# Weights of narrow products 64 bytes further in their buffers, buffers at two places mod 512, and one buffer for a norm's two values

## The chip, the cores and the metric

One NeuronCore of one Trainium2 chip. The metric is the device time of one execution in microseconds, lower is better; it is compared with the same kernel without the change, on the same chip.

## The reference

A trunk of two decoder layers over 512 tokens of width 1024, all in float32, batch 1, then a final RMS norm:

```python
def hybrid_layer(x, g_mix, w_in, sinks, w_a, w_b, w_out, g_mlp, w_up, w_down):
    h = rmsnorm(x, g_mix)
    z = h @ w_in                                   # (512, 1024) @ (1024, 4864)
    aq, ak, av, rq, rk, rv, rg, ga, gb = jnp.split(z, SPLIT_POINTS, axis=-1)
    ...
    ya = sliding_window_sink_attention(aq, ak, av, sinks) @ w_a
    ...
    r = chunkwise_retention(rq, rk, rv)
    ...                                            # per-head norm, swish gate
    yb = r.astype(x.dtype) @ w_b
    mixed = jax.nn.sigmoid(ga) * ya + jax.nn.sigmoid(gb) * yb
    x = x + mixed @ w_out
    h2 = rmsnorm(x, g_mlp)
    x = x + jnp.square(jax.nn.relu(h2 @ w_up)) @ w_down      # width 4096 inside
    return x
```

## The kernel before

**Products.** The activations stand transposed in SBUF: features on the 128 partitions, tokens along the free axis. Every float32 operand is split into two parts, `hi` (rounded to float32r) and `lo` (the rest), and a product is three matmuls, hi x hi, hi x lo and lo x hi, accumulated in one PSUM bank (`products`, lines 390 to 392; `wo` has its own three-matmul loop, line 1296). A matmul has a stationary operand of 128x128, which a separate weight load (PEld) brings into the array, and a moving operand of 128 partitions and 512 or 256 columns.

**Units of weights.** Weights come from HBM in units of 128 x 1024 float32. `load_until` loads a unit into a `raw` buffer (five of them), `split_until` splits it: ScalarE writes `hi` (line 338), VectorE writes `lo` (line 339). There are four `hi` and four `lo` buffers, taken in turn; `unit` keeps up to three units split ahead of the one in use. `unit_order` names the units in their order: `w_in`, `w_a`, `rv`, `w_b`, `wo`, `w_up`, `pair`, `block`, and at the very end `w_end`.

**Which width a unit serves.** Units of `w_in`, `w_a`, `w_b` and `w_up` are stationary, in slices of 128 columns, against 512 moving columns (`chunk`, `group`, `two_chunks`, the loop over `w_a`). Units of `rv`, `block` and `w_end` are themselves the moving operand, 512 columns at a time. Units of `wo` and `pair` are stationary against 256 moving columns: `output` (`wo`) and `pair` (the up projection but its first 512 columns) use a seven-product scheme over 2x2 halves, in which the moving operand is one half of the tokens. `pair` runs seven `multiply` calls of 4 x 3 matmuls, and two pairs stand behind one another, 168 matmuls of 256 columns; then comes `down` with 84 matmuls of 512 columns on `block` units. There are 14 pairs to a layer. `output` runs 7 x 48 matmuls of 256 columns to a layer.

**Where things lie in SBUF.** The pools follow one another and each tag has its place for the whole kernel. Byte addresses in a partition, from the allocation:

| tile | begins at | mod 512 | bytes |
|---|---|---|---|
| `x`, `xh`, `xl`, `r0` to `r7`, `ones`, ... | 2,176 and on | 128 | |
| `raw`, 5 buffers | 119,424 | 128 | 4,096 each |
| `hi`, 4 buffers | 139,904 | 128, all four | 4,096 each |
| `lo`, 4 buffers | 156,288 | 128, all four | 4,096 each |
| `acc` (pool `tmp`) | 172,672 | 128 | 2,048 |
| `t`, `sh`, `sl` | 174,720 | 128 | 2,048 each |
| `rstd` | 193,152 | 128 | 2,048 |
| `big`, 6 buffers | 195,200 | 128 | 4,096 each |
| small tiles; `columns` is the last but one | 219,776 | various | |
| `late` | 220,224 | 64 | 8,192 |

(The first value of `x`, 2,176, is a header of small values; the activations start 512 bytes on.) A weight slice of 128 columns is 512 bytes, a moving slice of 256 columns 1,024, so within a buffer all slices of 256 or 512 columns keep the buffer's place mod 512. `xh`, `xl`, the `r` tiles and `late` hold moving operands; the `r` tiles and `late` are dealt out in quarters by `Slots`. `late` is used again and again: as a ninth `r` tile in the first half of a layer, and for other things later.

**The two values of a norm.** `acc` is the sum of squares over the features, written by `squared_input` and read by `token_sums` on TensorE (line 561); `rstd` is the inverse root spread over the partitions, written by ScalarE in `Rms.finish` (line 609) and read by VectorE where results leave PSUM, last in `gate` (line 826). Each has a buffer of its own.

**What sets the order.** Each engine has its own queue, and waits on semaphores that the framework places from the tiles; SP issues the weight loads, POOL the sums of weights in DRAM and the adds to `y`. TensorE's order is that of the program: `unit` is called by the product that needs it and splits further ones ahead.

Of the kernel before, what the change touches and what calls it, by code (L numbers as in the profile page):

```python
# [10 lines left out]
F32 = mybir.dt.float32  # L11
F32R = mybir.dt.float32r
# [5 lines left out]
P = 128  # L18
T = 512
# [3 lines left out]
NB = T // P  # L23
# [21 lines left out]
N_BLOCK = 8  # L45
N_PAIR = 14
UNIT = 1024
WARM = 8
PACE = 0.8
DEEP = 3  # L50
# [2 lines left out]
SPLIT = 3  # L53
# [57 lines left out]
def view(slot):  # L111
    return slot[0][:, slot[1], :]
# [3 lines left out]
def decoder(ctx, tc, xT, x_first, w_in, w_rv, w_a, w_b, w_wo, w_up, w_pair, w_down, w_end, tables, decay, band, g_last, out):  # L116
# [4 lines left out]
    wpool = ctx.enter_context(tc.tile_pool(name="wpool", bufs=3))  # L121
    tmp = ctx.enter_context(tc.tile_pool(name="tmp", bufs=6))
    small = ctx.enter_context(tc.tile_pool(name="small", bufs=6))
# [4 lines left out]
    def f32(ap):  # L128
        return ap.bitcast(F32)
# [7 lines left out]
    def bank(pool, name):  # L137
        return pool.tile([P, T], F32, tag=pool.name, name=name)
# [27 lines left out]
    def halves(i):  # L166

        return (slice(0, UNIT // 2), slice(UNIT // 2, UNIT)) if i < 3 else (slice(0, UNIT),)

    def raw_tile():  # L170
        return wpool.tile([P, UNIT], F32, tag="raw", name="raw", bufs=5)

# [7 lines left out]
    def load_until(n):  # L180
        while state["loaded"] < min(n, len(order)):
            i = state["loaded"]
            layer, name, j = order[i][:3]
            if name == "pair":
                load_part(i)
            elif name == "block":
                load_block(i)
            elif name in MIXING:
                load_values(i)
            else:  # L190
                raws[i] = raw_tile()
                for at in halves(i):
                    queue = nc.scalar if i == 0 and at.start == 0 else nc.sync
                    source = w_end[j] if name == "w_end" else weights[name][layer, j]
                    queue.dma_start(raws[i][:, at], source[:, at])
                    if i < 3:
                        load_x()
            state["loaded"] += 1
# [3 lines left out]

    LEFT, RIGHT = slice(0, UNIT // 2), slice(UNIT // 2, UNIT)

    sums_up = [dram.tile([N_PAIR, P, UNIT], F32, name=f"sums_up{l}") for l in range(DEPTH)]
    sums_down = [dram.tile([N_BLOCK, P, 2 * UNIT], F32, name=f"sums_down{l}") for l in range(DEPTH)]
    sums_last = dram.tile([P, 2, UNIT], F32, name="sums_last")
    MIXING = {"rv": w_rv, "wo": w_wo}
# [67 lines left out]
    def add_part(i):  # L276
        if order[i][3] in (1, 2):
            last = raws.pop(i - 1)
            at = LEFT if order[i][3] == 1 else RIGHT
            nc.vector.tensor_tensor(raws[i][:, at], last[:, LEFT], last[:, RIGHT], ALU.add)  # L280
# [18 lines left out]
    def add_block(i):  # L299
        e, part = order[i][2:]  # L300
        if part in (2, 4) and e < N_BLOCK - 1:
            raws[i] = raws.pop(i - 2)
            nc.vector.tensor_tensor(raws[i], raws[i], raws.pop(i - 1), ALU.add)
# [10 lines left out]
    def add_values(i):  # L314
        part = order[i][2]
        if part in (2, 4):
            raws[i] = raws.pop(i - 2)
            nc.vector.tensor_tensor(raws[i], raws[i], raws.pop(i - 4), ALU.add)

    def split_until(n):  # L320
        while state["split"] < min(n, len(order)):
            i = state["split"]
            name, part = order[i][1], order[i][-1]
            if name in MIXING:
                add_values(i)
            load_until(i + AHEAD)
            if name == "pair":
                add_part(i)
            elif name == "block":
                add_block(i)  # L330
            raw = raws[i]
            hi = wpool.tile([P, UNIT], F32R, tag="hi", name="hi", bufs=SPLIT + 1)
            lo = wpool.tile([P, UNIT], F32R, tag="lo", name="lo", bufs=SPLIT + 1)
            for at in (LEFT,) if name == "pair" and part == 3 else halves(i):
                if i == 0 and at.start == 0:
                    nc.vector.tensor_copy(hi[:, at], raw[:, at])
                else:
                    state["high"] = nc.scalar.activation(hi[:, at], raw[:, at], AF.Copy).ins  # L338
                nc.vector.tensor_tensor(lo[:, at], raw[:, at], f32(hi[:, at]), ALU.subtract)  # L339
            kept = {  # L340
                "pair": part < 2,
                "block": name == "block" and part < 4 and order[i][2] < N_BLOCK - 1,
                **{n: name == n and order[i][2] < 4 for n in MIXING},
            }
            if not kept.get(name):
                raws.pop(i)
            parts[i] = (hi, lo)
            state["split"] += 1

    def unit(name, layer):  # L350
        i = state["next"]
        assert order[i][:2] == (layer, name), (order[i], layer, name)
        state["next"] += 1
        hold = state["hold"]
        split_until(i + SPLIT + 1 if hold is None else max(i + 1, min(hold, i + SPLIT + 1)))
        return parts.pop(i)
# [11 lines left out]
    warm = bank(ps_aux, "warm")  # L368
    for _ in range(WARM):
        nc.tensor.matmul(warm.rearrange("p (a b) -> p a b", b=P), ones, ones.unsqueeze(1).broadcast_to([P, 4, P]), start=True, stop=True)  # L370
# [172 lines left out]
    def square_sum(acc, src, first):  # L543
        if first:
            nc.scalar.activation(acc, src, AF.Square)
        else:
            sq = temp("sq")
            nc.scalar.activation(sq, src, AF.Square)
            nc.vector.tensor_tensor(acc, acc, sq, ALU.add)
# [22 lines left out]
    acc_of = {}  # L572
# [4 lines left out]

    def squared_input(k, which):
        if k == 0:
            acc_of[which] = tmp.tile([P, T], F32, tag="acc", name="acc", bufs=1)  # L580
        square_sum(acc_of[which], x[:, k, :], k == 0)

    class Rms:
# [18 lines left out]
            self.parts = sum_parts(wide)  # L602

        def finish(self):
            self.value = tmp.tile([P, T], F32, tag="rstd", name="rstd", bufs=1)
            ps = bank(ps_aux, "ssq")
            for i, part in enumerate(self.parts):
                nc.tensor.matmul(ps, ones, part, start=i == 0, stop=i == 1)
            nc.scalar.activation(self.value, ps, AF.Copy)
# [4 lines left out]
    def layer_body(layer):  # L614
# [40 lines left out]
        def squares():  # L655
            for k in range(KD):
                squared_input(k, g_mix)
# [474 lines left out]
        for u in range(4):  # L1132
            hi, lo = unit("w_a", layer)
# [146 lines left out]
        def output():  # L1280
# [35 lines left out]
            def put(i, j, ps, sign, kept=None):  # L1316
                for m in range(2):
                    n = 4 * i + 2 * m
                    v = x[:, n : n + 2, TOKENS[j]]
                    if kept:  # L1320
                        nc.vector.tensor_tensor(v, v, kept[m], ALU.add)
                    nc.vector.scalar_tensor_tensor(v, both(ps[m]), float(sign), v, ALU.mult, ALU.add)
                    for k in (n, n + 1):
                        if i:
                            at, col = TOKENS[j], g_mlp * KD + k
                            split(xh[:, k, at], xl[:, k, at], x[:, k, at], gain[:, col : col + 1])
                        elif j:
                            scaled_input(k, g_mlp)
                    if not i:
                        pace(v[:, 0, :])  # L1330
                if i == 0 and j:
                    for k in range(4):
                        squared_input(k, g_mlp)
                    for ks in (0, 2):
                        first_inputs(ks)
                elif i and not j:
                    for k in range(4, KD):
                        squared_input(k, g_mlp)
# [33 lines left out]
        u_two, u_two_slots = slots.four()  # L1372
        u_one = [slots.one() for _ in range(2)]
        first_hi, first_lo = (view(t).rearrange("p (a t) -> p a t", t=H) for t in u_one)
        columns = small.tile([P, 2 * NB], F32, tag="columns", name="columns", bufs=1)
        factor, negative = (columns[:, i * NB : (i + 1) * NB] for i in range(2))
        if last:
            sq = small.tile([P, 3 * NB], F32, tag="sq", name="sq", bufs=1)
# [242 lines left out]
        class Ending:  # L1621
# [74 lines left out]
            def first_weights(self):  # L1696
                with tc.issue_after(self.turned):
                    split_until(state["next"] + 1)
# [67 lines left out]

    scaled_input(0, 0)
    split_until(1)
    for u in (2, 3):
        for k in (2 * u - 3, 2 * u - 2):  # L1770
# [4 lines left out]
    for layer in range(DEPTH):  # L1775
        layer_body(layer)
# [164 lines left out]
```

## Time and profile before

| what | value |
|---|---|
| runs, device time | 1462.47, 1464.08, 1465.19 us, median 1464.08 |
| profiled execution, span | 1462.3 us |
| granted TensorE clock | 0.999 on the mean |
| TensorE (matmul), busy | 1450.0 us, 99% |
| TensorE, weight loads | 1265.4 us, 87% |
| VectorE | 1169.0 us, 80% |
| ScalarE | 969.0 us, 66% |
| GpSimd | 222.3 us, 15% |
| matmuls | 8041 |

The span is that of the profiled execution, from its first to its last instruction, and its time is taken as that span: the page gives no other, and the fastest of the three timed runs is 0.2 us above it. Matmuls are pipelined, so the duration of one holds its way through the array and is longer than the distance from its start to the next one's. Busy time of TensorE says little on its own, therefore; starts in the timeline say how fast products follow one another.

### The profile page before, as it was taken

How to read it: one execution, taken by the hardware profiler on the slowest of the kernel's cores; microseconds unless marked ns; L12 is line 12 of the kernel's file. 1: busy time of each engine (PE TensorE's matmuls, PEld its weight loads, DVE VectorE, ACT ScalarE, POOL GpSimd, SP SyncE). 2: the span in 40 equal slices, each digit the busy share in tenths (PEclk: the TensorE clock that was granted, in tenths of full speed). 3: DMA queues.
4: the chain of work that ended last, by engine and by line, in shares of the span. 5: the costliest groups of instructions: out<-in, count | busy, mean ns of one | idle time of the engine just before them, and what ended most of it. 6: DMA issues, size and time to landing. Idle time of an engine off the chain costs nothing.

```text
span 1462.3 us, 22150 instructions
## 1 busy us (share of the span) xinstructions
PE 1450.0 (99%) x8041; PEld 1265.4 (87%) x8041; DVE 1169.0 (80%) x1762; ACT 969.0 (66%) x1592; POOL 222.3 (15%) x329
## 2 busy tenths in 40 slices
PE   9999999999999999999999999999999999999998
PEld 7888888888988999999888888888889799999997
DVE  6978876876898888888778788687778988788885
ACT  6657556543687777777756575565437777777775
POOL 0011012112101111111201110112120111111120
PEclk9999999999999999999999999999999999999999
DMA  7598369899745777666955983797885477777664
GB/s 257 177 288 225 103 174 299 232 244 255 224 119 195 192 197 190 165 184 179 307 178 172 290 222 111 217 291 219 222 210 174 137 198 201 191 192 197 178 185 146
DMA packets 96428, 297.57 MB, mean 203 GB/s; under 512 B 11328, under 2 KB 11456, under 8 KB 90432
## 3 DMA queue, kind: packets, MB, share of 16 engines
q0 software_dynamic: 35936, 125.58, 37.2%
q1 hardware_dynamic: 59664, 169.27, 33.4%
q8 instruction: 63, 1.03, 0.3%
q10 hardware_dynamic: 720, 1.31, 0.2%
q14 instruction: 45, 0.37, 0.1%
HBM read 256.54 MB, written 115.87 MB: 255 GB/s over the span
## 4 chain that ended last, share of the span: by engine, by line
PE 96%; ACT 1%; DMA 1%; DVE 1%; issue 0%; DVEq 0%; ACTq 0%
PE mm L390 23%; PE mm L391 23%; PE mm L392 23%; PE wo L1296 5%; PE b L390 3%; PE b L391 3%; PE b L392 3%; PE rv L392 2%; PE rv L390 2%; PE rv L391 2%; PE mm L405 2%; PE score L773 1%; PE pT L738 1%; PE r L392 1%; PE r L391 1%; PE r L390 1%
## 5 line engine op out<-in xcount | busy, mean ns | idle before, releaser
L338 ACT ACTIVATE hi<-raw 128x1024 fp32r<-128x1024 f32 (+1 forms) x387 | 394.1, 1021 | 263.4 <-PE mm L391 146.9
L339 DVE TENSOR_TENSOR lo<-raw,hi 128x1024 fp32r<-128x1024 f32 (+1 forms) x388 | 452.7, 1174 | 107.4 <-ACT hi L338 105.3
L390 PE MATMUL mm<-xh,hi 128*128 128x512 f32 (+1 forms) x976 | 343.8, 356 | 1.8 <-ACT xh L413 1.0
L391 PE MATMUL mm<-xl,hi 128*128 128x512 f32 (+1 forms) x976 | 344.6, 356 | 0.0
L392 PE MATMUL mm<-xh,lo 128*128 128x512 f32 (+1 forms) x976 | 340.4, 355 | 0.0
L390 PEld LDWEIGHTS mm<-xh,hi 128*128 128x128 f32 x976 | 185.2, 190 | 27.7 <-ACT xh L413 1.7
L391 PEld LDWEIGHTS mm<-xl,hi 128*128 128x128 f32 x976 | 185.3, 190 | 24.2
L392 PEld LDWEIGHTS mm<-xh,lo 128*128 128x128 f32 x976 | 183.9, 190 | 23.6
L391 PE MATMUL mm<-r,hi 128*128 128x256 f32 (+1 forms) x608 | 189.2, 311 | 0.0
L392 PE MATMUL mm<-r,lo 128*128 128x256 f32 (+1 forms) x608 | 189.0, 311 | 0.0
L390 PE MATMUL mm<-r,hi 128*128 128x256 f32 (+1 forms) x608 | 186.6, 311 | 0.5 <-ACT mm L1471 0.5
L390 PEld LDWEIGHTS mm<-r,hi 128*128 128x128 f32 x608 | 115.8, 190 | 8.8 <-ACT mm L1471 0.7
L391 PEld LDWEIGHTS mm<-r,hi 128*128 128x128 f32 x608 | 115.8, 190 | 8.0
L392 PEld LDWEIGHTS mm<-r,lo 128*128 128x128 f32 x608 | 115.8, 190 | 6.3
L1619 POOL DMA_DIRECT2D y<-eu x56 | 62.4, 1354 | 374.4 <-DVE eu L1604 373.8
L391 PE MATMUL mm<-lo,r 128*128 128x512 f32 (+1 forms) x276 | 104.3, 387 | 0.0
L392 PE MATMUL mm<-hi,r 128*128 128x512 f32 (+1 forms) x276 | 101.3, 387 | 0.0
L390 PE MATMUL mm<-hi,r 128*128 128x512 f32 (+1 forms) x276 | 98.4, 390 | 0.9 <-ACT eu L1614 0.6
L390 PE MATMUL b<-hi,r 128*128 128x512 f32 x180 | 70.5, 392 | 1.6 <-DVE eu L1604 1.2
L391 PE MATMUL b<-lo,r 128*128 128x512 f32 x180 | 70.3, 390 | 0.0
L1296 PE MATMUL wo<-r,hi 128*128 128x256 f32 x384 | 69.4, 283 | 0.0
L392 PE MATMUL b<-hi,r 128*128 128x512 f32 x180 | 67.9, 390 | 0.0
(323 smaller groups left out, 2682.5 us busy)
## 6 DMA issues: line engine op xcount, KB each, us to landing
raw<-w_in_in SPq DMA_DIRECT2D x73, 512.0 KB, 5.8
sums_down<-w_down_in POOLq DMA_DIRECT2D x30, 1024.0 KB, 11.6
sums_up<-w_pair_in POOLq DMA_DIRECT2D x56, 512.0 KB, 10.9
raw<-w_down_in SPq DMA_DIRECT2D x45, 512.0 KB, 7.6
raw<-w_pair_in SPq DMA_DIRECT2D x84, 256.0 KB, 3.7
y<-y POOLq DMA_DIRECT2D x63, 256.0 KB, 9.4
y<-eu POOLq DMA_DIRECT2D x61, 256.0 KB, 8.1
raw<-sums_down SPq DMA_DIRECT2D x30, 512.0 KB, 7.4
```

What stands on the lines that cost most here:

```text
L338: state["high"] = nc.scalar.activation(hi[:, at], raw[:, at], AF.Copy).ins
L339: nc.vector.tensor_tensor(lo[:, at], raw[:, at], f32(hi[:, at]), ALU.subtract)
L390: nc.tensor.matmul(ps, ah, bh, start=start and i == 0, stop=False, **more)
L391: nc.tensor.matmul(ps, ah, bl, start=False, stop=False, **more)
L392: latest[0] = nc.tensor.matmul(ps, al, bh, start=False, stop=stop and i == n - 1, **more).ins
L405: latest[0] = nc.tensor.matmul(ps, w[:, cols(j, c)], moving[k][low], start=first, stop=bool(final)).ins
L738: nc.tensor.transpose(pt[:, i * P : (i + 1) * P], sm[:, at : at + P], ident)
L773: nc.tensor.matmul(ps[:, g * w : (g + 1) * w], q_s[g][:, c, at], part[:, keys], start=i == 0, stop=i == 1)
L1296: latest[0] = nc.tensor.matmul(o, w[:, cols], v, start=start and first and n % 2 == 0 and w is hi and v is vh, stop=final and w is lo, ski ...
L1619: nc.gpsimd.dma_start(y[:, 2 * j + m, i * T : (i + 1) * T], t, **how)
```

## The change

`hi` and `lo` buffers get 64 columns (256 bytes) more. A unit of `pair` or `wo` is put 16 columns (64 bytes) behind the start of its buffer, every other unit at its start. A buffer is then 4,352 bytes, so the four of a tag begin at 128, 384, 128 and 384 mod 512. `acc` and `rstd` share one buffer, `norm`, which frees 2,048 bytes, as many as the eight longer buffers take; `t` and all behind it to the small tiles keep their places mod 512. `columns` gets 16 columns (64 bytes) more that nothing uses, and `late`, the only thing behind it but a small tile, begins at 128 mod 512 in place of 64. The instructions and their number stay as they are.

```diff
+LINE = 16
+ASIDE = ("pair", "wo")
...
@@ split_until
             raw = raws[i]
-            hi = wpool.tile([P, UNIT], F32R, tag="hi", name="hi", bufs=SPLIT + 1)
-            lo = wpool.tile([P, UNIT], F32R, tag="lo", name="lo", bufs=SPLIT + 1)
+            aside = LINE if name in ASIDE else 0
+            hi, lo = (
+                wpool.tile([P, UNIT + 4 * LINE], F32R, tag=n, name=n, bufs=SPLIT + 1)[:, aside : aside + UNIT]
+                for n in ("hi", "lo")
+            )
@@ squared_input
         if k == 0:
-            acc_of[which] = tmp.tile([P, T], F32, tag="acc", name="acc", bufs=1)
+            acc_of[which] = tmp.tile([P, T], F32, tag="norm", name="acc", bufs=1)
@@ Rms.finish
-            self.value = tmp.tile([P, T], F32, tag="rstd", name="rstd", bufs=1)
+            self.value = tmp.tile([P, T], F32, tag="norm", name="rstd", bufs=1)
@@ layer_body
-        columns = small.tile([P, 2 * NB], F32, tag="columns", name="columns", bufs=1)
+        columns = small.tile([P, 2 * NB + LINE], F32, tag="columns", name="columns", bufs=1)
```

## The prediction

> **What bounds the kernel now.** I read the head of the profile page first, then the chain that ended last, then the groups of instructions with their shapes kept apart.
>
> ```profile
> span 1462.3 us, 22150 instructions
> ...
> PE 1450.0 (99%) x8041; PEld 1265.4 (87%) x8041; DVE 1169.0 (80%) x1762; ACT 969.0 (66%) x1592; POOL 222.3 (15%) x329
> ...
> PE 96%; ACT 1%; DMA 1%; DVE 1%; issue 0%; DVEq 0%; ACTq 0%
> ```
>
> TensorE (PE) is busy for 1450.0 of 1462.3 us and carries 96% of the chain: the kernel ends when its 8041 matmuls are through. An edit that adds or removes nothing can still move the time if it changes how fast one matmul follows the next. So the question is the distance from start to start, by width of the moving operand, and how many products of each width there are.
>
> ```profile
> L390 PE MATMUL mm<-xh,hi x976: 277/389/797, 5.8 to 1430.1; 128*128 128x512 f32 x129, 128*128 128x256 f32 x67
> L390 PE MATMUL mm<-r,hi x608: 277/283/397, 160.7 to 1437.1; 128*128 128x256 f32 x112, 128*128 128x512 f32 x40
> L390 PE MATMUL mm<-hi,r x276: 278/389/501, 429.4 to 1455.4; 128*128 128x512 f32 x134, 128*128 128x256 f32 x4
> L390 PE MATMUL b<-hi,r x180: 389/389/500, 436.3 to 1414.0; 128*128 128x512 f32 x180
> L390 PE MATMUL rv<-hi,r x64: 389/389/390, 189.4 to 950.1; 128*128 128x512 f32 x64
> ```
>
> ```profile
> L390 PE MATMUL mm<-r,hi 128*128 128x256 f32 x448 | 126.7, 283 | 0.5 <-ACT mm L1471 0.5
> ...
> L390 PE MATMUL mm<-xh,hi 128*128 128x256 f32 x336 | 94.6, 283 | 0.1
> ```
>
> ```profile
> L1296 PE MATMUL wo<-r,hi x384: 274/283/287, 366.3 to 1131.0; 128*128 128x256 f32 x192
> L1296 PE MATMUL wo<-r,lo x192: 278/283/286, 366.6 to 1131.1; 128*128 128x256 f32 x192
> L1296 PE MATMUL wo<-late,hi x64: 276/276/365, 395.1 to 1129.6; 128*128 128x256 f32 x64
> L1296 PE MATMUL wo<-late,lo x32: 276/276/281, 395.4 to 1129.7; 128*128 128x256 f32 x32
> ```
>
> The first fence is line 390 alone, with least/median/greatest ns; the second its 256-column groups; the third line 1296, the products of `wo`. In "out<-moving,weights" the weight operand is named last. Line 390 has two sisters, 391 and 392, with the same counts. So the 256-column products of `pair` number 3 x (448 + 336) = 2352, and those of `wo` with a moving operand in an `r` buffer 384 + 192 = 576. The 283 ns is a duration with its drain, not the pace. The pace stands in the timeline:
>
> ```profile
> 605.11 0.28 PE L391 MATMUL mm<-xl,hi 128*128 128x256 f32 x1
> ...
> 606.43 0.40 PE L390 MATMUL b<-hi,r 128*128 128x512 f32 x1
> ```
>
> Eleven products of 256 columns start between these two: 1.32 / 11 = 0.120 us each, with no idle time between.
>
> **The change part by part: the 64 bytes.** No instruction is added, removed or resized. What moves is where the weights stand relative to the moving operand. Before, every `hi` and `lo` buffer, `xh`, `xl` and all `r` buffers begin at 128 mod 512, and every slice that a 256- or 512-column product takes of them is a multiple of 512 bytes further: weights and moving operand are at distance 0 mod 512. One tile is the exception, and it is the row I rest on: `late` begins at 64 mod 512, so where it is the moving operand, the weights lie 64 bytes ahead of it. The change gives that same distance to `pair` and `wo`. What the trace says of `late` at 256 columns stands in the last two rows of `wo` above; at 512 columns it says:
>
> ```profile
> L390 PE MATMUL mm<-late,hi x32: 394/394/443, 297.4 to 1088.2; 128*128 128x512 f32 x32
> L391 PE MATMUL mm<-late,hi x32: 394/394/398, 297.7 to 1088.5; 128*128 128x512 f32 x32
> ```
>
> At 256 columns the median is 276 ns against 283; at 512 it is 394 against 389 (the `b` and `rv` rows). In starts:
>
> ```profile
> 395.11 0.40 PE L1296 MATMUL wo<-late,hi 128*128 128x256 f32 x2
> ...
> 395.47 0.39 PE L1296 MATMUL wo<-late,hi 128*128 128x256 f32 x2
> ...
> 397.85 0.39 PE L1296 MATMUL wo<-r,hi 128*128 128x256 f32 x2
> ```
>
> The first three of this run still take (395.47 - 395.11) / 3 = 0.120 us; the 21 after them (397.85 - 395.47) / 21 = 0.1133 us; all 24 together 0.1142. So the gain per product is 5.8 ns (mean with the start) to 6.7 ns (steady). I take 6.0: in `pair` the 256-column products come in unbroken runs of 168, so the start weighs less than in 24. And for 512 columns:
>
> ```profile
> 296.53 0.39 PE L392 MATMUL mm<-xh,lo 128*128 128x512 f32 x1
> ...
> 297.44 0.39 PE L390 MATMUL mm<-late,hi 128*128 128x512 f32 x1
> ...
> 299.54 0.39 PE L568 MATMUL ssq<-sh,ones 128*128 128x512 f32 x1
> ```
>
> Four products at distance 0 take 0.91 / 4 = 0.227 us each, nine with `late` 2.10 / 9 = 0.2333: the same distance costs a 512-column product 6 ns. The diff shifts `pair` and `wo` alone, whose stationary slices serve 256 columns only.
>
> Terms. `pair`: 2352 x 6.0 = 14.1 us (13.6 to 15.8). `wo`: 576 x 6.0 = 3.5 us on TensorE; the 96 with `late` keep their distance (below).
>
> **What the gain uncovers.** Faster products free `hi` and `lo` buffers sooner and ask for the next split sooner.
>
> ```profile
> 365.00:400.00 35.00, 35.00 (x290) 34.74 (x289) 31.40 (x38) 21.88 (x30) 6.45 (x10) 1.00 0.71 226
> 400.00:440.00 40.00, 39.84 (x206) 33.72 (x205) 37.26 (x55) 32.93 (x53) 0.84 (x1) 1.00 0.43 122
> 520.00:560.00 40.00, 40.00 (x257) 36.53 (x256) 33.13 (x43) 30.32 (x49) 7.05 (x8) 1.00 0.68 186
> ```
>
> ```profile
> ACT hi L338 <- PE mm L391: 146.9, 95, 4.5
> ```
>
> Columns of the first fence after the length: busy PE, PEld, DVE, ACT, POOL, then the granted clock (1.00), DMA share and GB/s; the second is a line of the waits (total us, times, longest). A block of two pairs and one `down` lasts some 39 us (168 x 0.120 + 84 x 0.227) and would be 1.0 us shorter; DVE, 33.13 of 40, goes from 83% to 85%, and ScalarE's splits wait 146.9 us for TensorE to free a buffer, so they have time to give. In `pair` the gain stays. In the `wo` stage (365 to 400) DVE is at 31.40 of 35 and in the stage behind it at 37.26 of 40, where TensorE waits a little already. There part of the gain may come back as a wait for `xh`; I count 2.0 of the 3.5 us (0 to 3.9).
>
> **The pad of `columns`.** Its 64 bytes carry `late` from 64 to 128 mod 512. The 3 x 32 products of 512 columns that read it against unshifted weights come to distance 0 (or 256): 96 x 6.3 ns = 0.6 us gained. Its 96 products in `wo` have moving operand and weights both 64 further: nothing.
>
> **The shared buffer `norm`.** It removes 2 KB, which the eight buffers' 256 bytes use up, so what lies behind keeps its place. Its cost would be a wait of one value for the other's last reader.
>
> ```profile
> L826 DVE TENSOR_TENSOR gb<-mm,rstd x16: 628/684/692, 289.2 to 1068.4; 128x512 f32<-128x512 f32 x16
> ```
>
> ```profile
> L545 ACT ACTIVATE acc<-x x4: 614/615/616, 5.7 to 1121.4; 128x512 f32<-128x512 f32 x4
> ```
>
> The last read of `rstd` begins at 1068.4, the next write of `acc` at 1121.4: 53 us of cover. The other way round `rstd` is computed from the token sums of `acc` and can't be early. Nothing; without that cover it would be one late ScalarE write ahead of the norm.
>
> **The two places 256 bytes apart.** A buffer is now 4352 bytes long, so every second one begins at 384 instead of 128 mod 512. No row shows a distance of 256 or 320. It touches two sets. (a) Half of the 256-column products get 320 instead of 64: they keep their full gain, or lose it (8.1 us, half of 14.1 + 2.0); that they turn slower than now, no row of this width shows. (b) Half of the 512-column products on `hi` and `lo`, as weights or as moving operand: in the rows of line 390, the 256-column ones taken off, 3 x (640 + 160 + 276 + 180 + 64) = 3960, and some 200 in smaller groups, so about 2080. The nearest row is the shift by 64, 6.4 ns, so the bounds are +13.3 and -13.3 us. I take 0 for both: the shifts the trace does show look periodic. Slices of the same weights 512 bytes apart cost the same, as the steady 0.120 over four different slices shows, and 64 bytes change the pace by a fixed 6 to 7 ns with opposite signs at the two widths, which looks like a short pattern of lines more than like one of 512 bytes. That is the weakest step, and both ends stay in the range.
>
> **Sum.** 14.1 + 2.0 + 0.6 = 16.7 us off the span of 1462.3. The timed runs have their median at 1464.08, 1.8 above the span; I carry that along: 1464.1 - 16.7 = 1447.4, say 1447. Own range of this case: 14.2 to 20.3 us, 1444 to 1450.
>
> **A rule that speaks against it.** The trace has two paces for one width (0.120 and 0.1133 us) that differ in nothing I can name but the tile. The Trainium skill, "TensorE: Matmul & The Clock Gate", section "Step-by-step: what each phase is for", says that TensorE has two independent read ports, one for the moving operand and one for weights, so that loading the next weights "doesn't steal SBUF read bandwidth from the running matmul". By that rule the place of weights can't matter and the sum is 0. The `late` rows don't agree with it. The same page's "Back-to-back issue gap" gives N/2.4 + 2.5 ns, 109.2 for 256 columns; as an estimate from that page, products that fell to it would save 2928 x 10.8 = 31.6 us. The trace shows neither width there.
>
> **The rivals.**
> - *512-column products pay at 256* (b at its upper bound, a gained in full). For: the one other distance shown costs them 6 ns. Against: no row at 256. 1447.4 + 13.3 = 1460.7.
> - *Only the unshifted places gain* (a lost, b at 0): 1447.4 + 8.1 = 1455.4. For: the `late` rows show one distance, 64. Against: what is said of the pattern above.
> - *Slower:* the pattern repeats only after 512 bytes, so at 320 the 256-column products gain nothing and at 256 the 512-column ones pay: 1447.4 + 8.1 + 13.3 = 1468.8. Given the first loss, it decides from (16.7 - 8.1) / 2080 = 4.1 ns per 512-column product.
> - *No effect:* the moving operand's own place, 64 mod 512, made `late` fast, not the distance; weights that move do nothing. For it: rows where both operands lie in `late`, at distance 0.
>
> ```profile
> L391 PE MATMUL ret<-late x8: 280/310/396, 188.4 to 941.0; 128*128 128x512 f32 x2, 128*128 128x384 f32 x2, 128*128 128x256 f32 x2, 128*128 128x128 f32 x2
> ```
>
>   Its longest, 396 ns, is the 512-column form, as slow as `late` against unshifted weights (394). Against: it stands in a stretch of changing widths, and there are two. Only the 0.6 us of the pad remain: 1463.5.
> - *More than forecast:* 256 helps the 512-column products (b at its lower bound): 1447.4 - 13.3 = 1434. For it speaks only that no row excludes it; no 512-column row is faster than 0.227.
>
> **How the numbers follow.** Chances: forecast 0.57, 512 pay 0.13, half gain 0.09, slower 0.06, no effect 0.08, more 0.07. The first three hold 0.79 and a little of the last lies beside them: 1440 to 1462. A measurement of this kernel tells about 0.2% (2.9 us) from no change. Faster: 0.57 + 0.09 + 0.07 and most of the 0.13, which ends at 1460.7 near the limit of 1461.2: 0.82. Within: 0.12. Slower: 0.06.
>
> **What would show it.** Median duration of `pair` and `wo` products at 276 in place of 283, and a pace of 0.113 to 0.114 in runs of 256 columns, for units in both places alike; if units alternate between two paces, the half-step matters. 512-column products at 0.227 everywhere; 0.233 in every second unit is the first rival. `mm<-late` of 512 columns at 389. A new wait of TensorE for `xh` in the `wo` stage would show how much of the 3.5 us came back. I am wrong if the pace hangs on the place and not on the distance, or if 256 bytes are no whole period.

## The result, and the profile after

Right in sign, half right in size. The changed kernel takes 1455.41 us (median of four runs, 1454.16 to 1457.31) against 1463.93 (1462.47 to 1465.19) for the kernel before beside it: a ratio of 0.9947 with the interval 0.9933 to 0.9961, 8.5 us faster, where 16.7 were forecast. That is outside the range that the forecast gave for its own case, 1444 to 1450. The number falls on the rival "only the unshifted places gain" (1455.4), but not for that rival's reason, as the starts will show.

The head of the page after, with the shares of the chain that ended last:

```profile
span 1455.2 us, 22150 instructions
...
PE 1443.0 (99%) x8041; PEld 1258.8 (87%) x8041; DVE 1167.0 (80%) x1762; ACT 969.2 (67%) x1592; POOL 222.6 (15%) x329
...
PE 94%; DMA 2%; ACT 2%; DVE 1%; issue 1%; SPq 0%; DVEq 0%; ACTq 0%
```

The span is 7.1 us shorter and TensorE's busy time 7.0 us, with the same 8041 matmuls: TensorE still bounds the kernel, and nothing else took over. The groups with their shapes kept apart (lines are five further than before):

```profile
L395 PE MATMUL mm<-r,hi 128*128 128x256 f32 x448 | 125.8, 281 | 0.5 <-ACT mm L1476 0.5
...
L395 PE MATMUL mm<-xh,hi 128*128 128x256 f32 x336 | 94.1, 282 | 0.1
```

Before, these means were 283 ns; 276 was forecast; they are 281 and 282. So the narrow products (those of 256 columns) did get faster, but not as fast as `late` had been. What that means in starts stands in TensorE's timeline of one block (start, duration):

```profile
525.83 0.40 PE L395 MATMUL b<-hi,r 128*128 128x512 f32 x1
...
528.58 0.28 PE L395 MATMUL mm<-r,hi 128*128 128x256 f32 x1
...
544.12 0.63 PE L395 MATMUL mm<-hi,r 128*128 128x512 f32 x2
544.60 0.28 PE L395 MATMUL mm<-r,hi 128*128 128x256 f32 x1
...
545.96 0.63 PE L396 MATMUL mm<-lo,r 128*128 128x512 f32 x2
```

Between the first two rows lie 12 products of 512 columns; then come 132 of 256 columns in 544.12 - 528.58 = 15.54 us, 0.1177 us each; then two of 512 columns; then 12 of 256 columns in 545.96 - 544.60 = 1.36 us, 0.1133 us each. All 144 narrow products have their weights 64 bytes from the moving operand. They run at two paces.

Over the whole trace, each matmul's time to the next start added up by kind (us, worked out from the starts of the two traces):

| kind | before | after | difference |
|---|---|---|---|
| `pair`, 256 columns (2352) | 284.53 | 279.54 | -4.99 |
| `wo`, 256 columns (672, `late` with them) | 80.51 | 79.25 | -1.26 |
| `late` at 512 columns (96) | 22.45 | 21.82 | -0.63 |
| other 512-column products with stationary `hi`, `lo` | 575.68 | 575.10 | -0.58 |
| `hi`, `lo` as the moving operand | 388.36 | 388.92 | +0.56 |
| all others | 103.08 | 102.94 | -0.14 |
| sum | 1454.6 | 1447.6 | -7.0 |

The sum explains the span. (The profiled execution is the longest of the four, 1457.31 us, so its 7.1 is less than the 8.5 of the medians; experiment 4's profile has a span of 1453.4.) Before, 2789 of the 3024 narrow products took 119 ns or more from start to start; after, 2445 take 116 to 118 and only 248 take 115 or less.

The rest went as the steps had it. `late`, with columns least/median/greatest ns:

```profile
L1301 PE MATMUL wo<-late,hi x64: 276/281/367, 393.8 to 1124.6; 128*128 128x256 f32 x64
L395 PE MATMUL mm<-late,hi x32: 389/389/442, 297.2 to 1083.9; 128*128 128x512 f32 x32
```

At 512 columns its median went from 394 to 389, as forecast. At 256 columns it went from 276 to 281, though its distance to the weights is still 64 bytes: the row on which the forecast rested lost its pace without any change of distance. The longest waits of TensorE, and the three windows of before again:

```profile
PE b L395 <- DVE eu L1609: 1.2, 1, 1.2
...
PE wo L1301 <- ACT xh L418: 0.2, 1, 0.2
```

```profile
365.00:400.00 35.00, 34.83 (x294) 34.54 (x293) 31.76 (x39) 22.55 (x32) 5.76 (x9) 1.00 0.73 227
400.00:440.00 40.00, 40.00 (x204) 33.82 (x204) 37.58 (x57) 33.01 (x52) 0.84 (x1) 1.00 0.42 121
520.00:560.00 40.00, 40.00 (x259) 36.46 (x258) 33.36 (x43) 31.44 (x52) 7.04 (x8) 1.00 0.68 184
```

No new wait of weight appears, TensorE is busy throughout at a granted clock of 1.00, and VectorE in its tightest stretch goes from 37.26 to 37.58 of 40.

### The profile page after: what moved, and what is told of

Read it like the earlier page. It is cut to its first block, busy times and chain, and to the rows that moved or that the text cites. A ratio compares the mean times of both kernels' runs of the same rounds, so it can differ in the third digit from the quotient of the medians.

```text
span 1455.2 us, 22150 instructions
## 1 busy us (share of the span) xinstructions
PE 1443.0 (99%) x8041; PEld 1258.8 (87%) x8041; DVE 1167.0 (80%) x1762; ACT 969.2 (67%) x1592; POOL 222.6 (15%) x329
## 4 chain that ended last, share of the span: by engine, by line
PE 94%; DMA 2%; ACT 2%; DVE 1%; issue 1%; SPq 0%; DVEq 0%; ACTq 0%
PE mm L395 23%; PE mm L396 23%; PE mm L397 22%; PE wo L1301 5%; PE b L395 2%; PE b L396 2%; PE b L397 2%; PE rv L396 2%; PE rv L395 2%; PE rv L397 2%; PE mm L410 2%; DMA raw<-w_pair_in 1%; PE score L778 1%; PE pT L743 1%; PE r L397 1%; PE r L396 1%
```

## The experiments

All start from the changed kernel.

**1. Is it the distance, or the weights' own place?** Two theories. A: the pace is set by the distance from moving operand to weights. B: by where the weights themselves lie. The map gives every unit, whatever its name, one of eight shifts, 0 to 224 bytes by 32, four units each; three sister kernels also move everything behind a first tile, both operands together, by 64, 128 or 192 bytes, with the same distances at other places.

```diff
-            aside = LINE if name in ASIDE else 0
+            aside = 8 * (i // 4 % 8)
```
```diff
-    little_x = const.tile([P, P + KD * T], F32, name="x")
+    little_x = const.tile([P, P + KD * T + 16], F32, name="x")      # 32, 48 in the other two
...
-    x = little_x[:, P:].rearrange("p (k t) -> p k t", t=T)
+    x = little_x[:, P : P + KD * T].rearrange("p (k t) -> p k t", t=T)
```

> The changed kernel with the weights' shift in the buffer going through 0, 32, 64, 96, 128, 160, 192, 224 bytes from unit to unit (each for four units in turn), for every kind of unit; the moving operands of pair and wo stay at 128 mod 512. A map of the pace over the weights' place. Theory A (the distance of weights and moving operand alone sets the pace, as I predicted): 0.120 us at shift 0 and one curve over the shift, which the three other maps must repeat; since the changed kernel showed 0.118 at 64, the 0.1133 of the old late rows must then turn up at another shift. Theory B (the places of the two operands each count, not only their distance): 0.120 at 0, 0.118 at 64, and no shift here gives 0.1133, because that came from the moving operand at 64 mod 128. 512-column products with stationary weights: A 0.233 at 64 as late had, B 0.227 to 0.230 at 64.

> The same cycle of shifts with everything behind the first tile 64 bytes further, so that the moving operands stand at 192 mod 256. Theory A: the same curve over the shift as the first map, 0.120 at 0 and 0.118 at 64. Theory B with a period of 128 bytes: the moving operand is at 64 mod 128, where late was, so the shift of 64 (weights at 0 mod 256) gives 0.1133 to 0.115 and a 512-column product there 0.233; with a period of 256, another value than the first map at some shift.

> The same with everything 128 bytes further (moving operands at 0 mod 256). Theory A: the first map's curve. Theory B with period 128: also the first map's curve; with period 256: another.

> The same with everything 192 bytes further: moving operands at 64 mod 256, the very place of the old late, and the shift of 64 puts the weights at 128 mod 256, the very place of the old hi and lo. Theory A: the first map's curve, 0.118 at 64. Theory B: 0.1133 to 0.115 at shift 64 for 256 columns and 0.233 for 512, whatever the period.

One run each: 1474.56, 1477.44, 1475.05 and 1476.74 us, beside 1463.86 before. The times only mix good and bad distances; the maps are read by start-to-start means, ns, by distance mod 256 bytes. These are those of the first map, from the seventh product of a stretch of one distance on, without pauses of TensorE; the second row is of stationary weights:

| distance | 0 | 32 | 64 | 96 | 128 | 160 | 192 | 224 |
|---|---|---|---|---|---|---|---|---|
| 256 columns | 120.0 | 118.1 | 115.4 | 119.3 | 118.7 | 119.8 | 117.8 | 117.6 |
| 512 columns | 226.9 | 233.4 | 233.4 | 234.1 | 232.5 | 233.2 | 230.1 | 233.3 |

The four maps give the same numbers within 0.4 ns, so A holds and B falls. Weights that are the moving operand themselves follow the 512-column row by their distance too. The forecast's steps "opposite signs at the two widths" and "256 bytes are a whole period" stand: no run shows a difference between the two places of a buffer.

But A alone doesn't give the time. It expected the 0.1133 us of `late` at another shift than 64, and they turn up at 64 itself, beside 0.118. There the mean, 115.4 ns, is no pace at all: the 10th, 25th, 50th, 75th and 90th percentile are 113, 113, 114, 118 and 118 in every map. TensorE's timeline of the first map shows both paces within 9 us:

```profile
492.95 0.40 PE L395 MATMUL b<-hi,r 128*128 128x512 f32 x1
...
495.75 0.28 PE L395 MATMUL mm<-r,hi 128*128 128x256 f32 x1
...
500.00 0.28 PE L395 MATMUL mm<-xh,hi 128*128 128x256 f32 x1
500.11 0.28 PE L396 MATMUL mm<-xl,hi 128*128 128x256 f32 x1
500.23 0.28 PE L395 MATMUL mm<-xh,hi 128*128 128x256 f32 x1
...
502.84 0.40 PE L397 MATMUL mm<-xh,lo 128*128 128x256 f32 x2
```

The first two rows bound 12 products of 512 columns at distance 224: 2.80 / 12 = 0.233 us. Behind them, 36 narrow products at 64 take 500.00 - 495.75 = 4.25 us, 0.118 each. The two rows at 500.00 and 500.11 are at distance 96. The next 23 starts, at 64 again, take 502.84 - 500.23 = 2.61 us, 0.1135 each. Same width and same distance; what differs is the unit of weights and what came just before, and each run kept its pace. Distance 64 isn't alone in this. The two halves of one unit at distance 192 differ too, in the same trace:

```profile
1263.79 0.28 PE L395 MATMUL mm<-xh,hi 128*128 128x256 f32 x1
...
1265.15 0.39 PE L395 MATMUL b<-hi,r 128*128 128x512 f32 x1
...
1267.94 0.28 PE L395 MATMUL mm<-r,hi 128*128 128x256 f32 x1
...
1269.35 0.28 PE L395 MATMUL mm<-r,hi 128*128 128x256 f32 x1
```

Twelve products take 1.36 us, 0.1133 each, and the next twelve, behind 12 products of 512 columns, 1.41 us, 0.1175 each. The three other maps show the same at this unit.

**2. Does the entry choose it? Distance 0 ahead of each long run.** Theory C: a run at 64 that is entered from narrow products at distance 0, as `late` was in the kernel before, takes the fast pace. Theory D: something else made `late` fast.

```diff
+def opens(u):
+    return u[3] == 0 and u[2] % 2 == 0 if u[1] == "pair" else u[2:] == (0, 0)
...
-            aside = LINE if name in ASIDE else 0
+            aside = LINE if name in ASIDE and not opens(order[i]) else 0
```

> The changed kernel, but the unit that opens each run of pair products (part 0 of the first pair of a block) and the first unit of wo lie at shift 0; all others at 64. Same instructions. Theory C (at distance 64 a run of 256-column products has two paces that keep themselves, 0.1133 and 0.1177 us, and what stands ahead of the run decides: a steady 512-column stretch at 0.227 leads into the slow one, products of 256 columns at distance 0 into the fast one, as in the old late rows): the opening 24 products of a block run at 0.120, the some 120 behind them at 0.1133; 14 blocks x 120 x 4.4 ns and 2 x 264 x 4.4 ns less, 16 x 24 x 2.2 ns more: 1455.4 - 7.4 - 2.3 + 0.8 = 1446.5. Theory D (the pace at distance 64 hangs on which tiles and buffers meet, and the late rows were fast for their place): only the shifted opening units change, 1456.2.

1457.13 us (1455.76 to 1457.83), ratio 0.996 (0.9946 to 0.9974). C missed by 10.6 us. TensorE's timeline in a block:

```profile
527.01 0.28 PE L400 MATMUL mm<-r,hi 128*128 128x256 f32 x1
...
528.44 0.28 PE L400 MATMUL mm<-r,hi 128*128 128x256 f32 x1
...
542.57 0.63 PE L400 MATMUL mm<-hi,r 128*128 128x512 f32 x2
```

The 12 opening products, at distance 0, take 1.43 / 12 = 0.119; the 120 behind them, at 64, take 14.13 / 120 = 0.1178. Distance 0 ahead isn't enough. It wasn't the same entry as `late` had, either: there the moving operand jumped to another place and the weights stayed, here the weights jump. Theory D's 1456.2 lies within the spread of these runs, which doesn't show it yet; experiment 7 tells.

**3. What do the places, the pad and the shared buffer cost by themselves?** No unit is shifted; all else of the change stays.

```diff
-ASIDE = ("pair", "wo")
+ASIDE = ()
```

> The changed kernel without the shift of pair and wo: longer buffers at two places mod 512, the shared norm buffer and the pad of columns stay. If those cost nothing (distance 256 is distance 0, the norm's wait is hidden): 256-column products at 0.120, 512-column ones at 0.227, late's 96 products of 512 columns gain 0.6 us and its 96 in wo lose 0.4: 1463.9. If the two places cost the 512-column products what 64 bytes do: up to 1477.

1463.57 us (1461.15 to 1464.48), ratio 0.9999 (0.999 to 1.0008). The groups with their shapes apart:

```profile
L395 PE MATMUL mm<-r,hi 128*128 128x256 f32 x448 | 126.6, 283 | 0.5 <-ACT mm L1476 0.5
```

The narrow products are back at 283 ns. The two places 256 bytes apart, `norm` and the longer `columns` together cost nothing that can be measured, and the gain of the change comes with the 64 bytes of `pair` and `wo`.

**4. The changed kernel once more.**

> The changed kernel itself, on the chip and in the call of the two above, to compare them with: 1455.4, 0.9947 of the kernel before.

1455.09 us (1454.6 to 1456.65), ratio 0.9947 (0.9934 to 0.9959): the first result again.

**5. A finer map.** Sixteen shifts by 16 bytes, of `pair` and `wo` alone.

```diff
-            aside = LINE if name in ASIDE else 0
+            aside = 4 * (i // 4 % 16) if name in ASIDE else 0
```

> The changed kernel with the shift of pair and wo units going through 0, 16, 32 ... 240 bytes, each for four units in turn; 512-column units at shift 0. A finer map of the 256-column pace. Theory C: more than one shift has two paces, the least of any shift stays near 0.113 (no distance is free of the loss), and shift 64 shows 0.1133 in runs entered from another 256-column distance and 0.1177 in those entered from a steady 512-column stretch. Theory D: one pace to a shift.

One run, 1459.99 us. In this cycle no unit of `pair` or `wo` comes to lie at 64, so what the expectation says of 64 wasn't tested here; the values for 64 are those of the first map. Steady means of long runs, ns, of both maps: 0: 120.0; 16 and 32: 118.3; 48: 117.8 or 123.3; 64: 113.4 or 117.8; 80: 118.6; 96: 117.4, 118.7 or 120; 112 and 144: 120; 160: 119.7 to 120.3; 176: 118.1; 192: 117.8; 208: 116.7; 224: 116.7 or 117.7; 240: 117.3. Several distances have more than one pace. The least in this run itself is 116.7, not the 113 that theory C expected. In long runs only 64 reaches 113.4. (The piece of 12 at 192 above did too, but no kernel here has its long runs at 192 in that pace, so whether 192 would serve as well is open.) The next two experiments enter 64 in another way.

**6 and 7. Another distance ahead of each long run.** The opening unit of two pairs, and the first of `wo`, at 96 or at 160 bytes; all others stay at 64.

```diff
-            aside = LINE if name in ASIDE else 0
+            aside = (24 if opens(order[i]) else LINE) if name in ASIDE else 0      # 40 in the second
```

> As the run with opening units at shift 0, but they lie at 96 bytes. In the map, each run at 64 that followed products of 256 columns at 96 went on at 0.1133, while shift 0 ahead led into 0.1177. Theory C (two paces that keep themselves; the distance ahead decides which): 120 products of each block and 264 of each wo stage at 0.1133: 1455.1 - 14 x 120 x 4.5 ns (7.6) - 2 x 264 x 4.5 ns (2.4) = 1445 us, ratio to before 0.987. Theory E (which pace comes hangs on what the engine did in the map's mixture, not on the 96 alone): 0.1177 as before, 1455 to 1457.

> The same with the opening units at 160 bytes. In the map 512-column products at 160 in their steady pace of 0.231 led into 0.1133, and after a few of them into 0.1177; 256-column products at 160 ahead of 64 were not seen. Theory C says one of the two paces and no third, kept through the run: 1445 to 1446 or 1455 to 1457, nothing between except the opening units themselves.

With 96: 1453.74 us (1452.02 to 1454.43), ratio 0.9933 (0.992 to 0.9947). It works in `wo` and not in `pair`:

```profile
368.04 0.39 PE L1306 MATMUL wo<-r,hi 128*128 128x256 f32 x2
...
371.44 0.39 PE L1306 MATMUL wo<-r,hi 128*128 128x256 f32 x2
...
526.82 0.28 PE L400 MATMUL mm<-r,hi 128*128 128x256 f32 x1
...
540.96 0.63 PE L400 MATMUL mm<-hi,r 128*128 128x512 f32 x2
```

In `wo` 30 products take 3.40 us, 0.1133 each. In `pair` 120 take 14.14, 0.1178 each. The opening products at 96 have no steady pace of their own: their last three starts ahead of the change to 64 are 116, 120 and 119 (or 117, 120, 118) ns apart in `wo`, 115, 119 and 116 (or 115, 118, 117) in `pair`. The same distance ahead, another phase of it, and another pace behind. That the phase decides is a reading of these rows; no run varies it alone. The number of opening products isn't it: 24 stand ahead of `wo`, 12 ahead of most runs of `pair`, but one run of `pair` has 22 ahead of it and is slow.

With 160: 1449.51 us (1447.61 to 1451.7), ratio 0.9904 (0.989 to 0.9917), 14.7 us below the 1464.16 of the kernel before beside it. The head, the groups and a block in the timeline:

```profile
span 1449.2 us, 22150 instructions
...
PE 1435.3 (99%) x8041; PEld 1249.9 (86%) x8041; DVE 1166.7 (81%) x1762; ACT 970.4 (67%) x1592; POOL 223.6 (15%) x329
```

```profile
L400 PE MATMUL mm<-r,hi 128*128 128x256 f32 x448 | 124.7, 278 | 0.5 <-ACT mm L1481 0.5
...
L400 PE MATMUL mm<-xh,hi 128*128 128x256 f32 x336 | 92.8, 278 | 1.0 <-ACT eu L1483 0.9
```

```profile
527.08 0.28 PE L400 MATMUL mm<-r,hi 128*128 128x256 f32 x1
...
528.51 0.28 PE L400 MATMUL mm<-r,hi 128*128 128x256 f32 x1
...
542.11 0.63 PE L400 MATMUL mm<-hi,r 128*128 128x512 f32 x2
```

The 12 opening products take 1.43 / 12 = 0.119 us each; the 120 behind them 13.60 / 120 = 0.1133. Nearly every long run is fast: 2411 narrow products take 115 ns or less, and `pair` sums to 273.92 us against 279.59 in experiment 4. By the ratios this kernel beats the kernel before and the changed one, and it differs from the changed kernel only in where one unit of every two pairs and the first unit of `wo` in a layer are put. The runs at 64 behind that unit have the same tiles and buffers in both kernels, so theory D falls. The fast pace can also be lost on the way: one run of 144 turns slow in the middle, behind a pause of TensorE that sets two starts 733 ns apart.

It stays 3.5 us above the upper end of its expectation, 1446. By the same sums, `pair` and `wo` keep back what the opening products (0.119) and the 12-product pieces that follow a steady run of 512 columns (0.1177 still) cost; and against experiment 4 the 512-column products with stationary weights are 1.9 us longer in sum, those with moving `hi` and `lo` 1.2, with a few waits of TensorE that were not there (the 0.9 us for `eu` in the group above is one). Two profiles of the changed kernel differ by 1.7 us in the first of these sums (575.10 and 573.43), so whether they are the price of the faster pace or chance of one execution, one profile can't say.

## Why the prediction was right in sign and wrong in size

- **What bounds it, and that only pace can move.** Right: the 7.0 us by kinds of products make up the span's 7.1.
- **Distance as the cause, and the rival "the moving operand's own place".** Right, and that rival falls: experiment 1 moves both operands through four places with the same curve.
- **"So the gain per product is 5.8 ns ... to 6.7 ns ... I take 6.0": this is the step that failed.** The gain is 4.99 us / 2352 = 2.1 ns in `pair`, and 1.38 / 576 = 2.4 in the products of `wo` that read an `r` tile. The terms were 14.1 and 2.0 (3.5 on TensorE); they came out at 5.0 and 1.4. The slow pace at 64 bytes, 0.1177, saves 2.3 ns on 0.120; the fast one, 0.1133, saves 6.7. The price was worked out on one run of 24 products with `late`, entered from narrow products at distance 0, an entry that the long runs of the changed kernel don't have.
- **"In `pair` the 256-column products come in unbroken runs of 168, so the start weighs less."** Wrong twice. The stretches are mostly 132 long with pieces of 12 apart, since `down` is woven in; and the start decides, it doesn't fade. Of 56 runs of 12 or more at 64 bytes that follow 512-column products in the changed kernel, the 43 that follow six or more start slow, and the 13 that follow two to four are fast. Two of the slow ones of 132, and the first of `wo`, turn fast on their way, each behind a pause of TensorE that sets two starts 333 or 448 ns apart; a run of 144 stays slow behind one of 739 ns.
- **The clue was in the trace of before**, in the rows of `wo` by `late` that the forecast didn't look through. The timeline of the second layer:

```profile
1124.71 1.03 PE L1259 MATMUL xt<-ident,x 128*128 128x128 f32 x8
1125.50 0.48 PE L1296 MATMUL wo<-late,hi 128*128 128x256 f32 x2
1125.82 0.28 PE L1296 MATMUL wo<-late,lo 128*128 128x256 f32 x1
...
1127.00 0.40 PE L1296 MATMUL wo<-r,hi 128*128 128x256 f32 x2
...
1128.80 0.39 PE L1296 MATMUL wo<-late,hi 128*128 128x256 f32 x2
...
1129.82 0.39 PE L1296 MATMUL wo<-r,hi 128*128 128x256 f32 x2
```

  From 1125.82 to 1127.00 ten products with `late` take 0.118 us each; from 1128.80 to 1129.82 nine take 0.1133. The first piece follows the turning of `x` by eight 128-column matmuls and a pause, the second follows narrow products. One tile, one distance, two paces, before anything was changed.
- **The half-step of 256 bytes at 0 for both widths, "the weakest step".** Right. Experiment 3 measures the places without the shift at 0.9999, and the maps repeat after 256 bytes. So the rival whose number came true, half the units gaining, is not what happened. Units in both places gain alike; leaving out pauses, the mean of `pair` goes from 119.7 to 117.5 ns in each.
- **`late` at 512 columns, 0.6 us.** Right, 0.63. **`norm`, nothing.** Right, with experiment 3.
- **Part of `wo`'s gain coming back as a wait for `xh`.** Not seen, 0.2 us as before. The gain was small; but in experiment 7, too, where `wo` gains its full size (80.51 to 77.01 us), the group of `wo` with `late` stands idle for 0.2 us only:

```profile
L1306 PE MATMUL wo<-late,hi 128*128 128x256 f32 x64 | 11.4, 279 | 0.2 <-DVE x L1332 0.2
```

  So 3.5 was the better term than 2.0, once the pace is had.
- **The rule that speaks against it.** The sentence of the Trainium skill ("TensorE: Matmul & The Clock Gate", "Step-by-step: what each phase is for") that loading weights doesn't take read bandwidth from the running matmul would make all distances equal. The maps disagree: 113.4 to 123.3 ns for 256 columns by the place of the weights alone.

What was shown is that distance gives the choice of paces, that what precedes a run chooses among them (experiments 4 and 7 differ in nothing else), and that the run keeps its choice while TensorE doesn't pause. Which property of the lead-in decides, and why there are two paces, inside the engine, was not measured. One sign only: in the slow pace at 64 bytes every third weight load lasts 192 ns and the others 187 or 188, in the fast one all last 187 or 188, and at distance 0 all last 192.

## What to carry to other kernels

Where TensorE is the bound and its products follow one another without idle time, read start-to-start times and not durations, and look at where the two operands lie relative to each other mod 256 bytes: here that and the place of the units that lead in, with no instruction changed, were worth up to 1%. Before a pace from a few rows is multiplied by thousands, look at every stretch of the same kind, at what leads into it, and whether the new stretches will be entered in the same way; a pace that has two values is not to be averaged. When a layout gives a part of what its best rows promise, try another lead-in before another layout.

## What the runs showed of the hardware

- Narrow products (256 columns, float32 in its rounded form) follow one another at 113.3 to 123.3 ns by the distance between weights and moving operand mod 256 bytes; 512-column ones at 226.9 to 234.1, with 0 the best. The best distance of one width is not that of the other: 64 bytes give 113.3 and 233.4, 0 gives 120.0 and 226.9.
- At 64 bytes there are two paces, starts 113, 113, 114 or 118, 117, 118 ns apart, each kept through runs of 120 to 288 products without a pause. Behind a pause of TensorE (two starts 216 ns apart or more) the pace can turn to the other, either way, or stay.
- After a change of width, 512-column products need six products to come back to their pace: 234, 236, 228, 233, 231, 227 ns and then 226 or 227. In the changed kernel, where these 512-column products lie at distance 0, narrow products at 64 behind two to four of them are fast; behind six or more, slow. In the maps, narrow products at 64 behind long stretches of 512-column products at 160 or 192 are fast as well, so it isn't the number of them alone.
